# The experts of a mixture layer: gather behind gate/up, scatter inside its group, one tile of gathered tokens, 22 places for weights

## Chip, cores and metric

The kernel runs on one NeuronCore of a Trainium2 chip. The metric is device time of one execution, in microseconds (us); the number to compare is the median of several executions. Engines: PE is TensorE (matrix products, PEld its weight loads), DVE is VectorE, ACT is ScalarE, POOL is GpSimd, SP is SyncE, which here only issues DMAs.

## What is computed

Two networks in a row on 256 tokens of width 1024, batch 1. The first has two layers of gated linear attention, forgetting attention and a convolutional feed-forward; the second has one layer of windowed attention and a recurrent mixer, and ends with a mixture of experts. Only the mixture matters here: 32 experts in 4 groups, each token picks a group and in it the best two experts, and every expert is a gated feed-forward of width 256.

```python
    e_w, e_idx = lax.top_k(jax.nn.softmax(e_sel, axis=-1), TOP_K)
    e_w = e_w / jnp.sum(e_w, axis=-1, keepdims=True)
    weights = (g_w * e_w).astype(h.dtype)
    expert = (g_idx * EXPERTS_PER_GROUP + e_idx).reshape(-1)
    ...
    hg = lax.ragged_dot(xs, w_gate, sizes)
    hu = lax.ragged_dot(xs, w_up, sizes)
    ys = lax.ragged_dot(jax.nn.silu(hg) * hu, w_down, sizes)
    ...
        y = hierarchical_moe(h, ...)
        x = x + ga2 * rmsnorm(y, ln2_post[l])
```

## The kernel before

All weights stream from HBM in loads of 1 MiB (128 x 2048 fp32). `stream_load` (L145) issues the next load of one list on SP's queue into a place; `stream_done` (L160) gives a place back when its weight has been used, and at once issues the next load into it. So loads go in list order, and a load waits for the release of the place that it takes. For the experts there are 21 places: 5 in `ring`, 10 in `ring2` (8 of them shared with buffers of the stage before), 5 in `ring3` (L1687) and 1 in `ring3b` (L1729). The expert list (L286) has 96 loads: per group gate, up and down of each expert. The very last down weight comes in four parts.

The 32 experts are worked in 11 groups (`GROUPS`, L267), p = 0 to 10, of two or four experts: pairs for p = 0 to 3, 5 and 7, quads for 4, 6, 8, 9 and 10 (`LAST`). The first eight experts are fixed, the others come in the order of their load, which SP reads from a register. In a pair an expert has up to 64 token places, in a quad 32, so a group fills 128 columns or rows. Should an expert have more tokens than places, `dense` (L1979) does the rest behind a branch; here it is skipped.

The schedule is written by hand (`manual_schedule`): every engine works in program order. A group p passes through these steps:

- `onehots(p)` (L1741): DVE and ACT make the 0/1 matrix from tokens to places (PQ, PR). It also takes the tile XG[p] for the gathered tokens, from two tiles "xg0" and "xg1" in turn.
- `gather(p, q)` (L1764), q = 0 and 1: 8 products (16 instructions) pick the group's tokens out of `xv` into one PSUM bank; then four scalings, ACT, DVE, ACT, DVE, write four of the eight k tiles of XG[p]. The bank is "g", of which there is one.
- `gate_up(p)` (L1795): products of gate, then of up, into bank "gu"; the hook `between` puts work behind a certain k. Then ACT's silu and DVE's product give sg.
- `down_1` (L1817): two transposes of sg into a bank "dn" (there are two), and DVE's copy hm.
- `places(p)` (L1778): transposes of PQ into bank "g", PT by ACT, and the places' weights ws by DVE.
- `down_2(p, hm)` (L1825): products of the down weights, 512 columns at a time; `parts` splits the scaled result into yh (ACT) and yl (DVE), each 1024 columns wide.
- `scatter(p)` (L1868): 8 products add yh and yl to four y banks, which stay through the whole stage. PSUM has 8 banks: four y, two "dn", one "gu", one "g".

The order on TensorE in the loop (L2039) for 0 < p < LAST: gate; gather(p+1, 0); half of up; gather(p+1, 1); the other half of up; three quarters of scatter(p-1); down_1's transposes; the last quarter of scatter(p-1); places(p+1); the down products. In group 0 the gathers stand elsewhere: places(0), gather(1, 0), down_1's transposes, gather(1, 1), the down products, places(1). `by_rank` (L1950), a row of small DVE operations, follows down_1 in group 1; `most_over` (L1974), a transpose into "g" and a reduction, follows group 3.

The last group works its four experts two by two, since their weights come last; before it stand the branch and the transposes of the output gain `gbrow`. `keep_warm` (L1703) issues dummy products; 40 of them stand before the last down products. These come in quarters of 256 columns, each followed by `parts` and by the scatter of the quarter before. Behind that the result is normalised: squares (`last_sq`, ACT), the gain (`last_gain`, DVE), the root (`post_r`, DVE and POOL), the sum with the residual (`last_sum`, three on DVE, one on ACT and POOL), and four stores.

Of the kernel before, what the change touches and what calls it, by code (L numbers as in the profile page):

```python
# [20 lines left out]
EPS = 1e-6  # L21
# [13 lines left out]
def kernel(ctx: ExitStack, tc: tile.TileContext, a: dict, out: bass.AP, dump=None):  # L35
# [124 lines left out]
    def stream_done(key):  # L160

        del W["tiles"][key]
        stream_load(W["from"].pop(key))
# [1563 lines left out]

    t3 = sb_pool("t3", "right")
    ring3b = sb_pool("ring3b", "right")  # L1729
    stream_load((ring3b, 1))  # L1730
    p3 = ctx.enter_context(tc.tile_pool(name="p3", bufs=1, space=PSUM))

    def c3(tag, bufs, shape, dtype=F32):
        return t3.tile([128] + list(shape), dtype, name=tag, tag=tag, bufs=bufs)
# [6 lines left out]
    def onehots(p):  # L1741

        n, x0 = len(GROUPS[p]), GROUPS[p][0]
        m = 128 // n
        PR[p] = c3("PR", 1, (2, 128))
        if p == 0:
            for i in range(2):
                for s in range(n):
                    dve.tensor_scalar(PR[p][:, i, m * s:m * s + m], it[:, 1, 0:m], pos[:, i, x0 + s:x0 + s + 1],
                                      ss[:, i, 7:8], op0=OP.is_equal, op1=OP.mult)  # L1750
        PQ[p] = c3("P", 2, (2, 128), F32R)
        ps_ = (pos if x0 < FIXED else posA)[:, :, x0:x0 + n]
        dve.tensor_tensor(PQ[p].rearrange("p i (a b) -> p i a b", a=n),
                          it[:, 1, None, None, 0:m].to_broadcast([128, 2, n, m]),
                          ps_[:, :, :, None].to_broadcast([128, 2, n, m]), op=OP.is_equal)
        for i in range(2) if p else ():
            r = ss[:, i, 7:8]
            if i:
                act.activation(PR[p][:, i], PQ[p][:, i].bitcast(F32), AF.Copy, scale=r)
            else:  # L1760
                dve.tensor_scalar(PR[p][:, i], PQ[p][:, i].bitcast(F32), r, None, op0=OP.mult)
        XG[p] = c3("xg%d" % (p % 2), 1, (8, 128))

    def gather(p, q, tag="g"):  # L1764
        pg = b3(tag, 2 if tag == "dn" else 1, (4, 128))
# [26 lines left out]
            r = slice(m * s, m * s + m)  # L1792
            dve.tensor_reduce(WS[p][r], pt[r, 256 + 2 * s:258 + 2 * s], axis=AX.X, op=OP.add)

    def gate_up(p, between):  # L1795
        n_ = len(GROUPS[p])
        m = 128 // n_
        pg = b3("gu", 1)

        for c0, n in ((0, "gate"), (256, "up")):  # L1800
            for s0 in range(0, n_, 2) if p == LAST else (0,):
                some = range(s0, s0 + 2 if p == LAST else n_)
                for k in range(8):
                    for s in some:
                        pe.matmul(pg[m * s:m * s + m, c0:c0 + 256], XG[p][:, k, m * s:m * s + m],  # L1805
                                  W["tiles"][3, n, GROUPS[p][s]][:, k * 256:k * 256 + 256], start=k == 0, stop=k == 7,
                                  skip_group_check=True)
                    if (n, k) in between:
                        between[n, k]()
                for s in some:  # L1810
                    stream_done((3, n, GROUPS[p][s]))
        sg = c3("sg", 1, (256,))
        act.activation(sg, pg[:, 0:256], AF.Silu)
        dve.tensor_tensor(sg, sg, pg[:, 256:512], op=OP.mult)
        return sg
# [8 lines left out]

    def down_2(p, hm):  # L1825
        m = 128 // len(GROUPS[p])
        yh, yl = c3("yh", 1, (1024,), F32R), c3("yl", 1, (1024,), F32R)
        YG[p] = (yh, yl)

        def products(pd, group, c0, c1):  # L1830
            pd = pd.rearrange("p (a b) -> p a b", b=256)
            for f in range(2):
                for s in group:
                    r = slice(m * s, m * s + m)
                    w = W["tiles"][3, "down", GROUPS[p][s]].rearrange("p (q f m) -> p q f m", q=4, f=2)
                    pe.matmul(pd[r], hm[:, f, r], w[:, c0 // 256:c1 // 256, f], start=f == 0, stop=f == 1,  # L1836
                              skip_group_check=True)

        def parts(pd, c0, c1):
            act.activation(yh[:, c0:c1], pd, AF.Copy, scale=WS[p])  # L1840
            dve.scalar_tensor_tensor(yl[:, c0:c1], pd, WS[p], yh[:, c0:c1].bitcast(F32), op0=OP.mult, op1=OP.subtract)  # L1841

        n = len(GROUPS[p])
        if p < LAST:
            for d in range(2):
                pd = b3("dn", 2)
                products(pd, range(n), d * 512, d * 512 + 512)
                parts(pd, d * 512, d * 512 + 512)
            for x in GROUPS[p]:
                stream_done((3, "down", x))  # L1850
            return

        pds = [b3(t, 2 if t == "dn" else 1) for t in ("dn", "dn", "gu", "g")]
        keep_warm(40, pds[0][:, 256:384])
        for q in range(4):
            products(pds[q][:, 0:256], range(n - 2), q * 256, q * 256 + 256)
        for q in range(4):
            products(pds[q][:, 0:256], range(n - 2, n), q * 256, q * 256 + 256)
            if q:
                scatter(p, range(4), q - 1)  # L1860
            parts(pds[q][:, 0:256], q * 256, q * 256 + 256)
            if q == 2:
                last_sq(0, 0), last_gain(0, 0)
        scatter(p, range(4), 3)

    LAST = len(GROUPS) - 1

    def scatter(p, some=range(4), q=None):  # L1868
        for c in some:
            i, d = c // 2, c % 2  # L1870
            if q is not None and d != q // 2:
                continue
            r = slice(0, 512) if q is None else slice(q % 2 * 256, q % 2 * 256 + 256)
            for n, part in enumerate(YG[p]):
                pe.matmul(y[i][d][:, r], PT[p][:, i * 128:(i + 1) * 128], part[:, d * 512 + r.start:d * 512 + r.stop],  # L1875
                          start=p == 0 and n == 0, stop=p == LAST and n == 1, skip_group_check=True)

    y = [[b3("y%d%d" % (i, d), 1) for d in range(2)] for i in range(2)]

# [22 lines left out]
    def ranks(step):  # L1902

        sq_ = [128, NV, NV]
        cmp = t3.tile(sq_, F32, name="cmp", tag="yh" if step else "yl", bufs=1) if step < 2 else W["cmp"]
        if step == 0:
            dve.tensor_tensor(cmp, key[:, None, :].to_broadcast(sq_), key[:, :, None].to_broadcast(sq_), op=OP.is_gt)
            dve.tensor_reduce(rank, cmp, axis=AX.X, op=OP.add)
# [70 lines left out]
    def dense():  # L1979
# [5 lines left out]
        dve.tensor_tensor(wov, pos, cap[:, None].to_broadcast([128, 2, 32]), op=OP.is_gt)  # L1985
        dve.tensor_tensor(wov, wov, wf, op=OP.mult)
        for i in range(2):
            h2T = t3.tile([128, 8, 128], F32, name="h2T", tag="xg%d" % (1 - LAST % 2), bufs=1)
            for k in range(8):
                z = t3.tile([128, 128], F32, name="z", tag="sg", bufs=1)  # L1990
                pz = b3("g", 1, (128,))
# [34 lines left out]
        tt[i, d] = W["res"][:, 2 * i + d].rearrange("p (a b) -> p a b", a=4)  # L2026
        dve.tensor_tensor(tt[i, d], y[i][d].rearrange("p (a b) -> p a b", a=4), gbrow[:, 4 * d:4 * d + 4], op=OP.mult)  # L2027

    def last_sum(i, d, eng):
        xd = xv[:, i, 4 * d:4 * d + 4]  # L2030
        if eng is pool:
            act.activation(tt[i, d], tt[i, d], AF.Copy, scale=ss[:, i, 3:4])
            pool.tensor_tensor(tt[i, d], tt[i, d], xd, op=OP.add)
        else:
            dve.scalar_tensor_tensor(tt[i, d], tt[i, d], ss[:, i, 3:4], xd, op0=OP.mult, op1=OP.add)  # L2035
        o = out[0, i * 128:(i + 1) * 128, d * 512:(d + 1) * 512].rearrange("p (a b) -> p a b", a=4)
        (act if d else sp).dma_start(o, tt[i, d])

    for p in range(len(GROUPS)):  # L2039
        if p == LAST:  # L2040
            most = nc.values_load(over[0:1, 0:1], min_val=0, max_val=256)
            with tc.If(most > 0):
                dense()

            gbrow = t3.tile([128, 8, 128], F32, name="gbrow", tag="xg%d" % (1 - p % 2), bufs=1)
            for q in range(2):
                pt = b3("g", 1, (4, 128))
                for c in range(4):
                    pe.transpose(pt[:, c], gains[:, 3, 4 * q + c:4 * q + c + 1].to_broadcast([128, 128]), ident)  # L2049
                act.activation(gbrow[:, 4 * q:4 * q + 4], pt, AF.Copy)  # L2050
        between = {}
        if 0 < p < LAST:
            onehots(p + 1)
            between = {("gate", 7): lambda: gather(p + 1, 0), ("up", 3): lambda: gather(p + 1, 1)}
        sg = gate_up(p, between)
        if p:
            scatter(p - 1, range(3))
        else:
            places(0), gather(1, 0, "dn")
        hm = down_1(sg)  # L2060
        if p:
            scatter(p - 1, range(3, 4))
        if p == 1:
            mx = by_rank()
        if p == 0:
            gather(1, 1)
        elif p < LAST:
            places(p + 1)
        down_2(p, hm)
        if p == 0:  # L2070
            places(1)
        if p == 3:
            most_over(mx)

    for i, d in ((1, 0), (0, 1), (1, 1)):
        last_sq(i, d)
    last_gain(1, 0)
    post_r(0, 0, True), post_r(1, 0, True)
    last_gain(0, 1)
    post_r(0, 0, False)  # L2080
    last_gain(1, 1)
    post_r(1, 0, False)
    last_sum(0, 0, dve), last_sum(0, 1, pool), last_sum(1, 0, dve), last_sum(1, 1, dve)


def _laid_out(v):
# [67 lines left out]
```

## Time and profile before

| what | value |
|---|---|
| median of 3 runs | 1057.34 us (1056.49 to 1057.43) |
| profiled execution, its own time | 1056.19 us |
| its span | 1054.4 us |
| PE busy | 1020.2 us (97%) |
| PEld busy | 901.8 us (86%) |
| DVE, ACT, POOL busy | 718.0 us (68%), 515.1 us (49%), 225.8 us (21%) |
| HBM read, mean rate | 246.23 MB, 235 GB/s |

The span is what the profiler saw of the program; the run's own time has some 1.8 us around it. A busy PE is not PE at its peak. In the timelines a row is a run of equal instructions: start, length, engine, line, operation, what it writes and reads, count, and in brackets how long its engine stood idle before it and what ended that. Products of fp32 count as two instructions. The granted clock of TensorE has two levels, shown as 1.00 (2.4 GHz) and 0.50 (1.2 GHz).

### The profile page before, as it was taken

Reading aid. Unit: us, or ns where it says so; the run is one execution under the profiler, and the core shown is the slowest. Engines: PE = TensorE matmul, PEld = TensorE weight load, DVE = VectorE, ACT = ScalarE, POOL = GpSimd, SP = SyncE. Lnnn points to the kernel's source line nnn. Section 1 sums busy time; section 2 is a strip of 40 time slices with the busy share of each in tenths; the row PEclk is TensorE's granted clock in tenths of the full one; section 3 lists DMA queues with packets and bytes.
Section 4 is the critical chain, followed back from the end, with each engine's and each line's share of the span. In section 5 each row is a group of like instructions: output and inputs, shape, how many; then the busy total and the mean of one; then the engine's idle time right before and its main releaser. Section 6 shows DMA issues by size and latency. Waiting matters only on the chain. (4 is left out here: it accounts for less than half of the span.)

```text
span 1054.4 us, 21292 instructions
## 1 busy us (share of the span) xinstructions
PE 1020.2 (97%) x8476; PEld 901.8 (86%) x8476; DVE 718.0 (68%) x1512; ACT 515.1 (49%) x914; POOL 225.8 (21%) x194
## 2 busy tenths in 40 slices
PE   8999999999999999999999999989999999999986
PEld 7989899999999998999999999988887766566543
DVE  6756778999988475677999999785666642222213
ACT  5554456666644554445666655566554322222212
POOL 2304122122112230322111213455323000000001
PEclk9999999999999999999999999999999999999988
DMA  8423155556678432334666659753258899999993
GB/s 326 171 81 120 59 210 206 211 215 225 231 259 317 176 137 81 121 120 163 234 214 249 224 218 343 276 211 123 82 203 353 352 350 364 390 419 420 420 420 142
DMA packets 36743, 248.69 MB, mean 236 GB/s; under 512 B 4240, under 2 KB 4672, under 8 KB 7840
## 3 DMA queue, kind: packets, MB, share of 16 engines
q1 hardware_dynamic: 35616, 245.53, 61.5%
q8 instruction: 68, 1.11, 0.4%
q10 hardware_dynamic: 864, 1.37, 0.4%
q0 software_dynamic: 160, 0.39, 0.1%
q14 instruction: 35, 0.29, 0.1%
HBM read 246.23 MB, written 1.05 MB: 235 GB/s over the span
## 5 line engine op out<-in xcount | busy, mean ns | idle before, releaser
L211 PE MATMUL mm<-xh,wh 128*128 128x272 f32 (+1 forms) x1192 | 348.6, 292 | 3.0 <-DVE raw L1491 1.3
L214 PE MATMUL mm<-xh,wl 128*128 128x272 f32 (+1 forms) x1192 | 341.0, 286 | 0.0
L212 PE MATMUL mm<-xl,wh 128*128 128x272 f32 (+1 forms) x1192 | 340.0, 285 | 0.0
L182 ACT ACTIVATE wh<-raw 128x1024 fp32r<-128x1024 f32 (+1 forms) x229 | 237.9, 1041 | 144.9 <-PE mm L212 85.8
L191 POOL TENSOR_TENSOR wl<-raw,wh 128x1024 fp32r<-128x1024 f32 (+1 forms) x68 | 164.1, 2413 | 487.1 <-ACT wh L182 472.7
L211 PEld LDWEIGHTS mm<-xh,wh 128*128 128x128 f32 x1192 | 225.7, 189 | 13.2 <-issue 11.1
L191 DVE TENSOR_TENSOR wl<-raw,wh 128x1024 fp32r<-128x1024 f32 (+1 forms) x162 | 196.1, 1213 | 44.0 <-ACT wh L182 42.8
L214 PEld LDWEIGHTS mm<-xh,wl 128*128 128x128 f32 x1192 | 225.9, 189 | 0.0
L212 PEld LDWEIGHTS mm<-xl,wh 128*128 128x128 f32 x1192 | 225.5, 189 | 0.0
L1805 PE MATMUL gu<-raw,xg 128*32 128x256 f32 (+1 forms) x1024 | 91.6, 392 | 2.1 <-DMA raw<-in_w_exp_up_dram 2.1
L1023 DVE SCALAR_TENSOR_TENSOR cv<-lg,vcol,cv 128x256 f32<-128x256 f32 (+2 forms) x168 | 81.8, 487 | 3.0
L1805 PEld LDWEIGHTS gu<-raw,xg 128*32 128x32 f32 (+1 forms) x1024 | 49.6, 122 | 38.4 <-issue 4.7
L211 PE MATMUL lg<-big,wh 128*128 128x272 f32 (+2 forms) x240 | 68.3, 285 | 0.0
L212 PE MATMUL lg<-big,wh 128*128 128x272 f32 (+2 forms) x240 | 68.2, 284 | 0.0
L214 PE MATMUL lg<-big,wl 128*128 128x272 f32 (+2 forms) x240 | 68.1, 284 | 0.0
L1774 DVE TENSOR_SCALAR xg<-g,gains,modT 128x128 f32<-128x128 f32 x40 | 16.4, 410 | 74.6 <-ACT xg L1776 74.6
L1012 ACT ACTIVATE cv<-lg,vcol 128x272 f32<-128x272 f32 (+1 forms) x84 | 47.5, 565 | 36.7 <-DVE lg L1010 36.5
L211 PE MATMUL mm<-big,wh 128*128 128x272 f32 (+2 forms) x208 | 59.4, 286 | 0.0
L212 PE MATMUL mm<-big,wh 128*128 128x272 f32 (+2 forms) x208 | 59.1, 284 | 0.0
L214 PE MATMUL mm<-big,wl 128*128 128x272 f32 (+2 forms) x208 | 59.0, 284 | 0.0
L1616 POOL TENSOR_TENSOR ss<-ss,nhalf 128x1 f32<-128x1 f32 x6 | 3.7, 624 | 233.2 <-DVE ss L1614 230.0
L1776 ACT ACTIVATE xg<-g,modT,gains 128x128 f32<-128x128 f32 x40 | 18.3, 458 | 68.6 <-PE g L1768 59.0
(538 smaller groups left out, 1771.3 us busy)
## 6 DMA issues: line engine op xcount, KB each, us to landing
raw<-in_w_up_dram SPq DMA_DIRECT2D x44, 1024.0 KB, 4.8
raw<-in_w_in_dram SPq DMA_DIRECT2D x34, 1024.0 KB, 4.8
raw<-in_w_exp_gate_dram SPq DMA_DIRECT2D x32, 1024.0 KB, 10.6
raw<-in_w_exp_up_dram SPq DMA_DIRECT2D x32, 1024.0 KB, 11.1
raw<-in_w_exp_down_dram SPq DMA_DIRECT2D x31, 1024.0 KB, 12.5
raw<-in_w_ada_dram SPq DMA_DIRECT2D x24, 1024.0 KB, 4.8
raw<-in_w_down_dram SPq DMA_DIRECT2D x16, 1024.0 KB, 5.7
raw<-in_w_out_dram SPq DMA_DIRECT2D x12, 1024.0 KB, 4.8
```

The source lines that it names most:

```text
L182: act.activation(wh, src, AF.Copy)
L191: eng.tensor_tensor(wl, src, wh.bitcast(F32), op=OP.subtract)
L211: pe.matmul(po, wh[:, k - off], xh[:, tsl], start=f, stop=False)
L212: pe.matmul(po, wh[:, k - off], xl[:, tsl], start=False, stop=False)
L214: pe.matmul(po, wl[:, k - off], xh[:, tsl], start=False, stop=e)
L1012: act.activation(t, hs[:, D0:NN], AF.Identity, bias=conv_bias(l, c), scale=conv_col(l, 2, c))
L1023: dve.scalar_tensor_tensor(o, i, conv_col(l, j, c), o, op0=OP.mult, op1=OP.add)
L1616: pool.tensor_tensor(ss[:, i, c + 3:c + 4], ss[:, i, c + 2:c + 3], nhalf[:, :1], op=OP.pow)
L1774: dve.tensor_scalar(XG[p][:, k], pg[:, c], g, bb, op0=OP.mult, op1=OP.add)
L1776: act.activation(XG[p][:, k], pg[:, c], AF.Identity, bias=bb, scale=g)
L1805: pe.matmul(pg[m * s:m * s + m, c0:c0 + 256], XG[p][:, k, m * s:m * s + m], W["tiles"][3, n, GROUPS[p][s]][:, k * 256:k * 256 + 256], star ...
```

## The change

- `ring3b` has two places instead of one (22 in all), and both are loaded at the start.
- XG is one tile "xg" for all groups. gather(p+1, 0) stands behind gate_up(p), ahead of down_1 and places(p+1); in group 0 places(0) stands ahead of it, now in the same bank "g".
- In `down_2` both "dn" banks are taken first; the first half is split into yh and yl (512 columns wide now, one tile each) between the products; then come scatter of the first half, `parts` of the second, gather(p+1, 1), scatter of the second half. The scatter of group p-1 inside group p is gone.
- In the last group 14 dummies stand behind gate/up in place of 40 before down_2; three quarters of the down products of the first two experts come ahead, the fourth is done with all four experts; the second half of yh and yl takes the tile "xg".
- `h2T` and `gbrow` move to a place of the ring that has become free; `cmp` in `ranks` is bf16.
- At the end the squares of the first halves come earlier, the root needs one DVE operation less behind the last square, and all four sums are on DVE.

```diff
-    stream_load((ring3b, 1))
+    for _ in range(2):
+        stream_load((ring3b, 2))
...
-        XG[p] = c3("xg%d" % (p % 2), 1, (8, 128))
+        XG[p] = c3("xg", 1, (8, 128))
...
-    def gate_up(p, between):
+    def gate_up(p):
...
-                    if (n, k) in between:
-                        between[n, k]()
...
         def parts(pd, c0, c1):
+            c0, c1 = c0 % 512, (c1 - 1) % 512 + 1
+            if c0 == 0 and p == LAST and p in YG:
+                both = c3("xg", 1, (2, 512), F32R)
+                YG[p] = [both[:, 0], both[:, 1]]
+            elif c0 == 0:
+                YG[p] = [c3(t, 1, (512,), F32R) for t in ("yh", "yl")]
...
         if p < LAST:
+            pds = [b3("dn", 2) for _ in range(2)]
             for d in range(2):
-                pd = b3("dn", 2)
-                products(pd, range(n), d * 512, d * 512 + 512)
-                parts(pd, d * 512, d * 512 + 512)
+                products(pds[d], range(n), d * 512, d * 512 + 512)
+                if d == 0:
+                    parts(pds[d], 0, 512)
             for x in GROUPS[p]:
                 stream_done((3, "down", x))
+
+            scatter(p, 0)
+            parts(pds[1], 512, 1024)
+            gather(p + 1, 1)
+            scatter(p, 1)
             return
...
-        keep_warm(40, pds[0][:, 256:384])
-        for q in range(4):
+        for q in range(3):
             products(pds[q][:, 0:256], range(n - 2), q * 256, q * 256 + 256)
         for q in range(4):
-            products(pds[q][:, 0:256], range(n - 2, n), q * 256, q * 256 + 256)
+            products(pds[q][:, 0:256], range(n - 2, n) if q < 3 else range(n), q * 256, q * 256 + 256)
             if q:
-                scatter(p, range(4), q - 1)
+                scatter(p, (q - 1) // 2, (q - 1) % 2)
             parts(pds[q][:, 0:256], q * 256, q * 256 + 256)
-            if q == 2:
-                last_sq(0, 0), last_gain(0, 0)
-        scatter(p, range(4), 3)
+            if q > 1:
+                last_sq(q - 2, 0), last_gain(q - 2, 0)
+        dve.tensor_scalar(ss[:, :, 2], ss[:, :, 0], 1.0 / 1024, EPS, op0=OP.mult, op1=OP.add)
+        scatter(p, 1, 1)
...
-        cmp = t3.tile(sq_, F32, name="cmp", tag="yh" if step else "yl", bufs=1) if step < 2 else W["cmp"]
+        cmp = t3.tile(sq_, BF, name="cmp", tag="yh" if step else "yl", bufs=1) if step < 2 else W["cmp"]
...
-            between = {("gate", 7): lambda: gather(p + 1, 0), ("up", 3): lambda: gather(p + 1, 1)}
-        sg = gate_up(p, between)
-        if p:
-            scatter(p - 1, range(3))
+        sg = gate_up(p)
+        if p == LAST:
+            keep_warm(14, b3("dn", 2, (128,)))
         else:
-            places(0), gather(1, 0, "dn")
+            if p == 0:
+                places(0)
+            gather(p + 1, 0)
         hm = down_1(sg)
-        if p:
-            scatter(p - 1, range(3, 4))
         if p == 1:
             mx = by_rank()
-        if p == 0:
-            gather(1, 1)
-        elif p < LAST:
+        if p < LAST:
             places(p + 1)
         down_2(p, hm)
-        if p == 0:
-            places(1)
...
-    last_sum(0, 0, dve), last_sum(0, 1, pool), last_sum(1, 0, dve), last_sum(1, 1, dve)
+    last_sq(0, 1), last_sq(1, 1)
     last_gain(0, 1)
...
+    for i in range(2):
+        dve.scalar_tensor_tensor(ss[:, i, 3:4], ss[:, i, 1:2], 1.0 / 1024, ss[:, i, 2:3], op0=OP.mult, op1=OP.add)
+        pool.tensor_tensor(ss[:, i, 3:4], ss[:, i, 3:4], nhalf[:, :1], op=OP.pow)
+        if i == 0:
+            last_gain(1, 1)
+    for i in range(2):
+        for d in range(2):
+            last_sum(i, d)
```

## Rows read from the trace of the kernel before

**Rows 1.** Windows: us; busy of PE, PEld, DVE, ACT, POOL; PEclk, DMA share, GB/s.

```profile
846.30:899.15 52.85, 52.68 (x381) 34.05 (x380) 18.67 (x59) 13.05 (x29) 0.00 (x0) 1.00 0.92 353
916.75:987.17 70.42, 70.17 (x668) 43.97 (x668) 20.55 (x54) 17.45 (x36) 0.00 (x0) 1.00 1.01 420
987.17:1009.69 22.52, 20.39 (x210) 11.47 (x202) 5.30 (x15) 4.36 (x9) 0.00 (x0) 0.92 1.02 421
```

**Rows 2.** SP queue's waits, 846 to 910, then 920 to 1005: total, times, longest.

```profile
SPq L155 <- PE gu L1805: 22.6, 7, 5.6
...
SPq L155 <- DMA raw<-in_w_exp_down_dram: 13.9, 11, 1.5
```

**Rows 3.** Timeline of TensorE, group 2 (863.85 to 881.34 us).

```profile
863.85 3.62 PE L1805 MATMUL gu<-raw,xg 128*64 128x256 f32 x32
867.40 2.05 PE L1768 MATMUL g<-PR,hT 128*128 128x128 f32 x16
...
875.24 0.50 PE L1875 MATMUL y<-yh,PT 128*128 128x512 f32 x1
...
876.74 0.38 PE L1820 MATMUL dn<-ident,sg 128*128 128x128 f32 x2
...
877.43 0.38 PE L1784 MATMUL g<-ident,P 128*128 128x128 f32 x2
...
877.86 3.65 PE L1836 MATMUL dn<-raw,hm 128*64 128x512 f32 x16
881.34 3.62 PE L1805 MATMUL gu<-raw,xg 128*64 128x256 f32 x32
```

**Rows 4.** Timeline of all engines in group 0, around gather(1, 0).

```profile
837.89 2.03 PE L1768 MATMUL dn<-PR,hT 128*128 128x128 f32 x16
...
838.47 0.33 DVE L1793 TENSOR_REDUCE ws<-g 64x1 f32<-64x2 f32 x2
...
839.96 0.46 ACT L1776 ACTIVATE xg<-dn,modT,gains 128x128 f32<-128x128 f32 x1 [1.52 <-PE dn L1768]
...
841.39 0.41 DVE L1774 TENSOR_SCALAR xg<-dn,gains,modT 128x128 f32<-128x128 f32 x1 [0.53 <-ACT xg L1776]
841.72 0.41 DVE L1822 COPY hm<-dn 128x256 f32<-128x256 f32 x1
...
842.23 0.65 PE L1836 MATMUL dn<-raw,hm 128*64 128x512 f32 x2 [0.31 <-issue]
```

**Rows 5.** Timeline of DVE in group 1: by_rank's first operation, and both yl behind it.

```profile
860.01 0.16 DVE L1952 COPY proc<-it 128x8 f32<-128x8 f32 x1
...
864.13 1.43 DVE L1841 SCALAR_TENSOR_TENSOR yl<-dn,ws,yh 128x512 fp32r<-128x512 f32 x2
```

**Rows 6.** Timeline of TensorE: waits of an earlier stage, and those of group 9.

```profile
700.25 0.36 PE L211 MATMUL mm<-xh,wh 128*128 128x258 f32 x1 [0.34 <-DVE raw L1491]
...
702.97 0.65 PE L1217 MATMUL at<-ident,gains 128*128 128x128 f32 x4 [1.04 <-DVE gains L1205]
...
993.60 0.62 PE L1805 MATMUL gu<-raw,xg 128*32 128x256 f32 x2 [0.25 <-DMA raw<-in_w_exp_up_dram]
996.09 3.34 PE L1805 MATMUL gu<-raw,xg 128*32 128x256 f32 x26 [1.87 <-DMA raw<-in_w_exp_up_dram]
```

**Rows 7.** Windows of TensorE alone: us; busy; PEclk, DMA share, GB/s.

```profile
996.50:999.80 3.30, 3.30 (x27) 0.50 1.02 425
```

**Rows 8.** The chain that ended last, from the last group on.

```profile
1016.26 13.92 PE gu L1805 x128
1030.18 1.59 PE y L1875 x6
...
1032.46 2.25 PE dn L1706 x40
1034.71 1.85 PE dn L1836 x16
...
1047.67 1.75 DVE raw L2035
```

More of the change, by code (lines that the diff above doesn't have):

```diff
@@ L1826, in down_2 @@
         m = 128 // len(GROUPS[p])
-        yh, yl = c3("yh", 1, (1024,), F32R), c3("yl", 1, (1024,), F32R)
-        YG[p] = (yh, yl)
         def products(pd, group, c0, c1):
@@ L1839, in parts @@
         def parts(pd, c0, c1):
+            c0, c1 = c0 % 512, (c1 - 1) % 512 + 1
[4 more added lines that the diff above has]
+                YG[p] = [c3(t, 1, (512,), F32R) for t in ("yh", "yl")]
+            yh, yl = YG[p]
             act.activation(yh[:, c0:c1], pd, AF.Copy, scale=WS[p])
@@ L1859, in down_2, with scatter @@
             if q:
-                scatter(p, range(4), q - 1)
+                scatter(p, (q - 1) // 2, (q - 1) % 2)
             parts(pds[q][:, 0:256], q * 256, q * 256 + 256)
-            if q == 2:
-                last_sq(0, 0), last_gain(0, 0)
-        scatter(p, range(4), 3)
+            if q > 1:
+                last_sq(q - 2, 0), last_gain(q - 2, 0)
+        dve.tensor_scalar(ss[:, :, 2], ss[:, :, 0], 1.0 / 1024, EPS, op0=OP.mult, op1=OP.add)
+        scatter(p, 1, 1)
     LAST = len(GROUPS) - 1
[L1868 to L1873, printed above, removed]
+    def scatter(p, d, q=None):
+        r = slice(0, 512) if q is None else slice(q * 256, q * 256 + 256)
+        for i in range(2):
@@ L1874, in scatter @@
             for n, part in enumerate(YG[p]):
-                pe.matmul(y[i][d][:, r], PT[p][:, i * 128:(i + 1) * 128], part[:, d * 512 + r.start:d * 512 + r.stop],
-                          start=p == 0 and n == 0, stop=p == LAST and n == 1, skip_group_check=True)
+                pe.matmul(y[i][d][:, r], PT[p][:, i * 128:(i + 1) * 128], part[:, r], start=p == 0 and n == 0,
+                          stop=p == LAST and n == 1, skip_group_check=True)
     y = [[b3("y%d%d" % (i, d), 1) for d in range(2)] for i in range(2)]
@@ L1987, in dense @@
         for i in range(2):
-            h2T = t3.tile([128, 8, 128], F32, name="h2T", tag="xg%d" % (1 - LAST % 2), bufs=1)
+            h2T = spare[:, 0:1024].rearrange("p (a b) -> p a b", a=8)
             for k in range(8):
@@ L2027, in last_gain, with last_sum @@
         dve.tensor_tensor(tt[i, d], y[i][d].rearrange("p (a b) -> p a b", a=4), gbrow[:, 4 * d:4 * d + 4], op=OP.mult)
-    def last_sum(i, d, eng):
+    def last_sum(i, d):
         xd = xv[:, i, 4 * d:4 * d + 4]
[L2031 to L2035, printed above, removed]
+        dve.scalar_tensor_tensor(tt[i, d], tt[i, d], ss[:, i, 3:4], xd, op0=OP.mult, op1=OP.add)
         o = out[0, i * 128:(i + 1) * 128, d * 512:(d + 1) * 512].rearrange("p (a b) -> p a b", a=4)
@@ L2040 @@
         if p == LAST:
+            spare = raw_tile(*R1)
             most = nc.values_load(over[0:1, 0:1], min_val=0, max_val=256)
@@ L2043 @@
                 dense()
-            gbrow = t3.tile([128, 8, 128], F32, name="gbrow", tag="xg%d" % (1 - p % 2), bufs=1)
+            gbrow = spare[:, 1024:2048].rearrange("p (a b) -> p a b", a=8)
             for q in range(2):
@@ L2050 @@
                 act.activation(gbrow[:, 4 * q:4 * q + 4], pt, AF.Copy)
-        between = {}
         if 0 < p < LAST:
             onehots(p + 1)
-            between = {("gate", 7): lambda: gather(p + 1, 0), ("up", 3): lambda: gather(p + 1, 1)}
-        sg = gate_up(p, between)
-        if p:
-            scatter(p - 1, range(3))
-        else:
-            places(0), gather(1, 0, "dn")
+        sg = gate_up(p)
+        if p == LAST:
+            keep_warm(14, b3("dn", 2, (128,)))
+        else:
+            if p == 0:
+                places(0)
+            gather(p + 1, 0)
         hm = down_1(sg)
-        if p:
-            scatter(p - 1, range(3, 4))
         if p == 1:
             mx = by_rank()
-        if p == 0:
-            gather(1, 1)
-        elif p < LAST:
+        if p < LAST:
             places(p + 1)
         down_2(p, hm)
-        if p == 0:
-            places(1)
         if p == 3:
             most_over(mx)
[L2075 to L2078, printed above, removed]
+    last_sq(0, 1), last_sq(1, 1)
     last_gain(0, 1)
-    post_r(0, 0, False)
-    last_gain(1, 1)
-    post_r(1, 0, False)
-    last_sum(0, 0, dve), last_sum(0, 1, pool), last_sum(1, 0, dve), last_sum(1, 1, dve)
+    for i in range(2):
[3 more added lines that the diff above has]
+            last_gain(1, 1)
+    for i in range(2):
+        for d in range(2):
+            last_sum(i, d)
 def _laid_out(v):
```

## The prediction

> **What bounds the kernel now.** I read the page first, then the experts' stretch (830 to 1054 us) by windows, then the DMA queue's waits, then TensorE's timeline of one group, then the timeline around the one place in the old kernel where the new order already occurs, and last the chain that ends the span.
>
> The windows show two regimes [rows 1]. In the pair groups (846 to 899 us) TensorE is busy without a break, 52.68 of 52.85 us, and the DMA moves 353 GB/s; from 917 us it moves 420 GB/s, its full rate here, while TensorE is still busy, 70.17 of 70.42 us. The queue's waits say the same: first SP waits for TensorE to release a place, later for earlier transfers [rows 2]. So the stage is close to balanced: a load of 1.05 MB costs 2.5 us at 420 GB/s, a pair group of six loads 15 us; one group costs TensorE 17.5 us (863.85 to 881.34) [rows 3]. TensorE first runs out of weights in group 9, which takes 22.52 us instead of 17.5 [rows 1, 3]. These 5.0 us are all the slack that TensorE has; what it loses beyond them moves the end.
>
> How it stays busy is seen in one group [rows 3]: a quarter gather of eight products (two of them per group, 2.0 us each) is cut into gate/up, and the up products behind it hide what ACT and DVE do with its result.
>
> **The 22nd place.** One load more in front is worth at most 2.5 us of DMA, and only where the DMA sets the end. It costs one issue on SP's queue, with nothing urgent behind it. I count it at nothing, because by the next part TensorE sets the end.
>
> **Gather behind gate/up.** Group 0 of the old kernel has this order once [rows 4]. The gather starts at 837.89 and ends 2.03 us later, at 839.92. Its four tiles are then scaled by ACT and DVE in turn (they read one PSUM bank, and each starts when the one before has ended): the first at 839.96, the fourth at 841.39, ended at 841.80, which is 1.88 us after the gather. Only then does DVE, in program order, copy hm (841.72 to 842.13), and the down products start at 842.23, 2.31 us after the gather's end. There a second gather of 2 us covers this, and 0.31 us of idle time is left [rows 4]. In the new order no second gather stands there. Behind the gather TensorE has two transposes (0.22 us), then places(p+1), whose transposes need the same bank "g" (one buffer), thus wait for the fourth scaling, and then the products, which wait for hm. With places at 0.43 us [rows 3] the products start 1.93 + 0.43 = 2.36 us after the gather; TensorE works 0.65 of it. **The new idle time is 1.71 us in each of groups 0 to 9, 17.1 us together.** I see nothing that takes this gap: sg is ready during the gather, and everything else stands behind the products in TensorE's order.
>
> In group 0 places(0) comes ahead of gather(1,0) in the same bank, so the gather waits for DVE's ws (838.47 + 0.33) instead of starting at 837.89: +0.95 us; the old 0.31 us goes [rows 4].
>
> **Scatter by halves in the group.** The number of products is the same. The first half waits for yl of the first half; ACT and DVE need some 1.5 us for it (a pass of DVE is 0.72 us, two take 1.43 [rows 5], and ACT's is about as long), beside the second half's products, 1.8 us of the 3.5 [rows 3]: nothing. The second yh reuses the first's tile and so waits for the first scatter, but gather(p+1,1), 2.0 us, stands between: nothing. The scalings behind that gather are covered by the second scatter (four products, 1.0 us: six take 1.5) and by the first four k of gate (1.8 us of 3.55) [rows 3]: nothing. Two exceptions. In group 1 DVE has by_rank in front of yl: from 860.01 to 864.13 [rows 5], 4.1 us, begun as hm's copy ends, so yl(0) ends about 4.6 us behind the products' start where scatter's second product wants it at 3.8: +0.8 us. In group 3 most_over's transpose needs bank "g" right behind the second scatter, 1.0 us before the scalings are through: +1.0 us. Group 9's own scatter, 2.0 us of work (1.59 us for six of eight [rows 8]), moves from the last group into group 9: +2.0 us there, and less behind.
>
> **One xg tile** costs nothing by itself: its first new write comes after gate/up has been read to the end. bf16 for cmp shortens work of DVE that nobody waits for: nothing.
>
> **Start of the last group.** 17.1 + 0.95 - 0.31 + 0.8 + 1.0 + 2.0 = 21.5 us more on TensorE, less the 5.0 us that it no longer waits for weights: +16.5 us. Weights are there by then. Their stream is delayed only up to the first release of group 4 (some 6.5 us, an estimate from the same terms, with one place more counted in); behind it the queue is full. The branch ahead of the last group and its own gate/up (6.57 us from 1009.69 to 1016.26, then 13.92 us [rows 1, 8]) stay as they are.
>
> **The last group.** From the end of gate/up (1030.18) to the first down products at 1034.71 it takes 4.53 us now: eight scatter products, transposes, forty dummies of 2.25 us [rows 8]. The new path has 14 dummies (14 x 0.056 = 0.8 us) over sg, transposes 0.2 us, and hm in 0.8 us (an estimate: a copy of 0.41 us [rows 4] and the hand-overs): 1.8 us, so -2.7 us. The first two experts' products fall from four quarters to three, -0.9 us; the last quarter takes all four experts at once, about +0.1 us, and a wait for scaling that used to be covered by work is a little longer, +0.2 us. Sum -3.3 us. In the old kernel these weights landed as they were needed; now they are there early, so nothing takes that back.
>
> **The end.** One sum went over ACT and POOL; beside it DVE's sum took 1.75 us [rows 8] against 0.72 us for a pass of that width with POOL at rest [rows 5]. Four sums in a row on DVE, with squares begun a step earlier: between 0 and -1.5 us, I take -0.8.
>
> **The clock.** After 1.87 us of waiting in group 9, with 0.25 us of idle time shortly ahead of it, 26 products took 3.34 us [rows 6] at a granted clock of 0.50, the 1.2 GHz level [rows 7]; at 2.4 GHz they take 26/64 of 3.6 us, 1.5 us. So a fall costs 1.9 us. A wait of 1.04 us with 0.34 us ahead of it [rows 6] was followed by products at full speed. The new gap of 1.7 us lies between 2.12 and 1.38, a little nearer to the second. Ends: none of ten gaps falls (0) or all do (19 us). I take one, +2 us.
>
> The Trainium skill ("TensorE: Matmul & The Clock Gate", section "Why this matters for your kernels") lets the clock fall only after a whole window of idle time; by that rule this term is 0 and the sum 2 us smaller. Group 9's row disagrees, since TensorE had worked 0.62 us between its two waits there, and the row decides.
>
> **Sum.** +16.5 - 3.3 - 0.8 + 2 = +14.4 us on the profiled execution's 1056.19 us: 1070.6. That execution lay 1.15 us under the median of the runs, 1057.34, so the median to expect is 1071.7, called 1072.
>
> **Rivals.**
> *The gap is covered and the DMA sets the end* (faster): if ACT and DVE scale while the gather runs, or in parallel, the down products start on time. Then the 22nd place gives its 2.5 us, the last group 3.3 and the tail 0.8: 1050.7 us. It decides from a gap under 0.26 us (4.4 us of other losses + ten gaps - 5.0 - 4.1 = -2.1). For it: ACT and DVE are idle most of the stretch. Against: all of the old kernel's gathers show the alternation, and with it even the 2 us cover left 0.31 us [rows 4]. Chance 0.10.
> *The clock falls at many of the gaps* (slower still): five to ten falls cost 9.5 to 19 us instead of 2: 1080 to 1089 us. For it: idle time of group 9 in a similar amount did it [rows 6, 7]. Against: a kept clock after 1.04 us. Chance 0.22.
> *The gap is there, but a third as long* (0.6 us), for instance because places gets its bank early: then the extra work is about the slack plus the last group's gain, 21.5 - 11 - 5.0 = 5.5, less 4.1: 1058.7, about the same. Chance 0.05.
> *The change doesn't do what it says*: the second load of the ring lands later than assumed. While TensorE sets the end this moves nothing; it is in the forecast.
>
> **Numbers.** Forecast as summed 0.63, with the rivals 0.22, 0.10 and 0.05. The forecast's own range is 1066 to 1076 (clock 0 to 3 falls, tail and exceptions). Taken to 1063 and 1084 it leaves out the faster rival and the upper half of the clock's. A measurement can tell 0.2%, 2.1 us, from no change: faster 0.11, same 0.03, slower 0.86.
>
> **What would show it.** Right: in each of groups 1 to 9 TensorE idle about 1.7 us between down_1's transposes and places' transposes, released by the fourth scaling; a pair group of about 19.2 us; no wait for weights in group 9; the first gate product of the last group near 1033 us; its down products 1.8 us behind gate/up. Wrong: groups of 17.5 us still, waits for weights at the end, or a granted clock of 0.5 behind most gaps.

## Result, and the profile after

The changed kernel takes 1069.82 us (median of 4 runs, 1067.67 to 1072.07) beside 1057.0 us for the kernel before on the same chip: ratio 1.0123, 95% interval 1.0098 to 1.0148. It is slower, 1072 was forecast, inside the range. The profiled execution took 1067.73 us with a span of 1066.0, 11.6 us more than the span before.

The windows of the changed kernel, one line for each of groups 0 to 9 (us; busy of PE, PEld, DVE, ACT, POOL; PEclk, DMA share, GB/s):

```profile
830.73:851.18 20.45, 17.76 (x132) 11.75 (x131) 9.21 (x29) 5.20 (x11) 0.00 (x0) 1.00 0.94 378
851.18:871.88 20.70, 18.92 (x127) 11.69 (x126) 8.19 (x32) 4.37 (x9) 0.00 (x0) 0.92 0.80 307
871.88:892.60 20.72, 18.95 (x127) 11.69 (x126) 4.84 (x13) 4.37 (x9) 0.00 (x0) 0.92 0.80 304
892.60:914.59 21.99, 19.20 (x128) 11.77 (x127) 5.62 (x16) 4.82 (x10) 0.00 (x0) 0.92 0.80 305
914.59:933.57 18.98, 17.20 (x207) 10.71 (x207) 4.61 (x12) 3.91 (x8) 0.00 (x0) 1.00 0.85 341
933.57:954.28 20.71, 18.93 (x128) 11.69 (x127) 5.14 (x15) 4.37 (x9) 0.00 (x0) 0.92 1.01 422
954.28:973.27 18.99, 17.22 (x207) 10.71 (x207) 4.84 (x13) 4.37 (x9) 0.00 (x0) 1.00 1.01 420
973.27:992.28 19.01, 17.23 (x128) 11.29 (x127) 5.12 (x15) 4.37 (x9) 0.00 (x0) 1.00 1.01 420
992.28:1011.26 18.98, 17.21 (x208) 10.71 (x207) 5.13 (x15) 4.37 (x9) 0.00 (x0) 1.00 1.01 419
1011.26:1032.02 20.76, 18.96 (x207) 11.03 (x206) 5.22 (x15) 4.36 (x9) 0.00 (x0) 0.92 1.01 419
```

A group that took 17.5 us [rows 1, 3] takes 19.0 where the clock stays at 1.00 (groups 4, 6, 7, 8) and 20.7 where the mean is 0.92 (1, 2, 5, 9; group 3 has most_over's wait besides). PE is idle some 1.8 us of each line: TensorE is no longer busy without a break. In groups 1 to 3 the DMA moves 305 GB/s, where it moved 353 [rows 1]: places come free later (from 846 to 910 us SP's queue waits 48.9 us for TensorE's releases, before it was 39.7).

TensorE's waits in the changed kernel, 830 us to the end (engine, line, waited for: us in total, times, longest):

```profile
PE g L1785 <- DVE xg L1775: 17.8, 10, 1.8
PE g L2053 <- DVEq L2046: 1.7, 1, 1.7
PE g L1983 <- DVE xg L1775: 1.0, 1, 1.0
PE g L1769 <- DVE ws L1794: 0.9, 1, 0.9
PE g L2053 <- ACT raw L2054: 0.7, 1, 0.7
PE dn L1832 <- DVE hm L1821: 0.5, 1, 0.5
```

The first line is the whole stall: ten times 1.78 us, at the transposes of places, released by the last scaling of the gather. No wait for weights is left.

The timeline of all engines in group 2 of the changed kernel shows how the gap comes about:

```profile
878.94 2.05 PE L1769 MATMUL g<-PR,hT 128*128 128x128 f32 x16
...
880.83 0.38 PE L1819 MATMUL dn<-ident,sg 128*128 128x128 f32 x2
881.09 0.46 ACT L1777 ACTIVATE xg<-g,modT,gains 128x128 f32<-128x128 f32 x1 [1.62 <-PE g L1769]
881.58 0.41 DVE L1775 TENSOR_SCALAR xg<-g,gains,modT 128x128 f32<-128x128 f32 x1 [1.66 <-ACT xg L1777]
882.03 0.46 ACT L1777 ACTIVATE xg<-g,modT,gains 128x128 f32<-128x128 f32 x1 [0.48 <-DVE xg L1775]
882.52 0.41 DVE L1775 TENSOR_SCALAR xg<-g,gains,modT 128x128 f32<-128x128 f32 x1 [0.53 <-ACT xg L1777]
882.85 0.41 DVE L1821 COPY hm<-dn 128x256 f32<-128x256 f32 x1
...
882.99 0.44 PE L1785 MATMUL g<-ident,P 128*128 128x128 f32 x2 [1.77 <-DVE xg L1775]
...
883.18 0.36 PE L1787 MATMUL g<-w,P 128*128 128x4 f32 x2
```

Four scalings pass the bank from engine to engine, ACT, DVE, ACT, DVE, with hm behind the last, as in group 0 before [rows 4]; only the work that stood beside them is gone. What follows is slow here:

```profile
883.47 5.35 PE L1832 MATMUL dn<-raw,hm 128*64 128x512 f32 x16
888.75 0.50 PE L1882 MATMUL y<-yh,PT 128*128 128x512 f32 x1
```

The sixteen down products behind the gap take 5.35 us; they took 3.65 [rows 3]. In five of the ten groups the granted clock fell to its 1.2 GHz level at that place (in group 3 it is 0.52 from 904.20 to 907.50 us, in group 4 it is 1.00 from 926.17 to 929.70), 1.70 us each, 8.5 us together; behind the five other gaps, of the same length, it stayed at 2.4 GHz.

Where the 11.6 us of span lie, from the two timelines: the stage starts 0.3 later; groups 0 to 9 take 201.3 us (830.73 to 1032.0) instead of 179.3 (830.41 to 1009.69), +22.0; from there to the last gate/up 3.6 instead of 6.5, -2.9; the last gate/up 11.5 instead of 13.9, -2.4; from its end to the last scatter's end 11.0 instead of 14.3, -3.3; the rest 7.9 instead of 10.0, -2.1.

### The profile page after: what moved, and what is told of

The parts are those of the page before. It is cut to its first block, busy times and chain, and to the rows that moved or that the text cites. A ratio compares the mean times of both kernels' runs of the same rounds, so it can differ in the third digit from the quotient of the medians.

```text
span 1066.0 us, 21229 instructions
## 1 busy us (share of the span) xinstructions
PE 1018.4 (96%) x8450; PEld 899.6 (84%) x8450; DVE 716.9 (67%) x1512; ACT 514.4 (48%) x913; POOL 224.6 (21%) x193
## 5 line engine op out<-in xcount | busy, mean ns | idle before, releaser
L1806 PE MATMUL gu<-raw,xg 128*32 128x256 f32 (+1 forms) x1024 | 82.7, 380 | 0.0
L1813 DVE TENSOR_TENSOR sg<-sg,gu 128x256 f32<-128x256 f32 x11 | 4.6, 422 | 70.5 <-ACT sg L1812 70.5
L1832 PE MATMUL dn<-raw,hm 128*32 128x512 f32 (+2 forms) x256 | 48.7, 658 | 0.5 <-DVE hm L1821 0.5
```

## The experiments

Nine kernels. All medians stand beside the kernel before on the same chip.

**The two holds, one at a time and both.** The gap may come from the PSUM bank "g" (places needs it) or from DVE's order (hm behind the scalings).

a_hm_first (picked and scaled are the two halves of gather):

```diff
-            gather(p + 1, 0)
+            pg = picked(p + 1, 0)
         hm = down_1(sg)
+        if p < LAST:
+            scaled(p + 1, 0, pg)
```

> The changed kernel, with the copy of hm put ahead of the scalings of gather(p+1, 0); the transposes of the places still write the PSUM bank that the gather has just filled. Theory (two holds of about equal length on TensorE, the bank and hm, one behind the other): the places still wait until VectorE has scaled the last slice out of that bank, so the idle stretch stays at 1.5 to 1.8 us in each of groups 0 to 9, groups without a fall of the clock last 18.8 to 19.1 us, and the time is 1066 to 1072 us. Rival (the order on VectorE alone makes the gap): it shrinks to under 0.4 us, groups last about 17.4 us, and the time is 1050 to 1055 us.

b_places_dn:

```diff
-        pt = b3("g", 1, (256 + 2 * n,))
+        pt = b3("dn", 2, (256 + 2 * n,))
```

> The changed kernel, with the transposes of the places in the other PSUM bank, which the gather does not use; the copy of hm stays behind the scalings on VectorE. Theory: the places follow down_1 at once, and the idle stretch moves to the first down products, which wait for hm: still 1.4 to 1.8 us in each of groups 0 to 9, 1066 to 1072 us. Rival (the bank alone makes the gap): under 0.4 us, groups of about 17.4 us, 1050 to 1055 us.

c_both, the two together, with by_rank behind the scalings:

```diff
-            gather(p + 1, 0)
+            pg = picked(p + 1, 0)
         hm = down_1(sg)
-        if p == 1:
-            mx = by_rank()
         if p < LAST:
             places(p + 1)
+            scaled(p + 1, 0, pg)
+        if p == 1:
+            mx = by_rank()
```

> The changed kernel with the chain behind the gather taken out of TensorE's way: the gather's products, then down_1 with hm's copy, then places(p+1) in a bank "dn", and only then the four scalings. Theory (the exposed chain and the clock falls behind it cost the time): the idle time behind down_1 falls from 1.77 us to under 0.4 us, no granted clock of 0.50 between groups 1 and 9, a group takes 17.5 to 17.8 us, and the DMA sets the end again: 1047 to 1051 us. Rival (scatter inside the group, with its waits, is what costs): groups still take 18.5 us or more, 1060 to 1070 us. Rival (the DMA lost its rate through late releases): TensorE waits for weights in groups 8 to 10, 1055 us or more.

Measured: a 1069.08 us (two executions; 1.0108, 1.0088 to 1.0128), b 1060.38 (1.0027, 1.0015 to 1.0039), c 1054.19 (0.9967, 0.9953 to 0.9981). TensorE's waits from 830 us on, first a:

```profile
PE g L1790 <- DVE xg L1780: 17.7, 10, 1.8
```

then b:

```profile
PE dn L1832 <- DVE hm L1821: 18.2, 11, 1.8
```

then c:

```profile
PE y L1887 <- DVE yl L1849: 2.4, 1, 2.4
PE dn L1837 <- DVE hm L1826: 2.3, 11, 0.5
PE gu L1811 <- DMA raw<-in_w_exp_up_dram: 1.9, 1, 1.9
...
PE dn L1837 <- DMA raw<-in_w_exp_down_dram: 1.5, 1, 1.5
```

With either hold taken away the idle time stays at ten times 1.77 us: in a it stays at the transposes of places, in b it moves to the down products, which wait for hm. With both away 0.18 us a group is left and groups last 17.26 us. The gap is two holds of equal length one behind the other: removing one leaves it as long as it was. c is faster than the kernel before, though above the 1047 to 1051 expected: by_rank now holds yl in group 1 (2.40 us, and the clock falls there), and from group 9 on weights are late.

The time expected of b was missed by 6 us with its gap as expected. Its clock fell behind two of the ten gaps only, those that end at 842.27 and 862.85 us; the four falls of a are one fewer than in the changed kernel. The spans of the changed kernel and b differ by 6.6 us (1066.0 and 1059.4). Groups 0 to 9 take 7.0 us less in b: three falls fewer are 5.1 us, and the rest are groups that are shorter by some 0.16 (a quad without a fall lasts 18.82 against 18.98) and ws, which holds TensorE for 0.65 us in group 1 instead of 0.92 in group 0. The medians differ by 9.4, since two of the changed kernel's four executions stand at 1072 us and b's profiled one is its slowest.

**The clock alone.** e_fill puts dummies in the gap:

```diff
         if p < LAST:
+            keep_warm(30, b3("dn", 2, (128,)))
             places(p + 1)
```

> The changed kernel with 30 dummies (1.7 us) between down_1's transposes and places(p+1) in groups 0 to 9, so the gap stays as long but TensorE isn't idle in it. Theory (gaps cost 1.77 us each, and in addition 1.7 us where the clock falls behind one): no fall of the clock from group 1 to 9, groups of 19.0 us, by_rank's wait of some 0.8 us appears in group 1; 1059 to 1063 us, with less spread between executions. Rival (falls have another cause): falls as before, 1067 to 1072 us.

Measured: 1060.61 us (1.0037, 1.0024 to 1.0049); the theory held. Groups 1 and 2 of e_fill by windows:

```profile
851.20:871.06 19.86, 19.17 (x158) 13.01 (x156) 8.20 (x31) 4.37 (x10) 0.00 (x0) 1.00 0.89 335
871.06:890.09 19.03, 18.93 (x158) 13.01 (x156) 4.83 (x12) 4.36 (x10) 0.00 (x0) 1.00 0.81 313
```

Group 2 lasts as long as a group of the changed kernel without a fall, 19.03 us: the gap itself costs the same whether TensorE idles or works in it, and what dummies can give back is the clock, 1.00 on average from 830 to 1030 us: 9.2 us of the median, and 7.8 of the span (1066.0 to 1058.2), which is the five falls' 8.5 less 0.8 that comes to light in group 1. Group 1 is 0.83 us longer than group 2: this is by_rank's delay, which the half clock had covered in the changed kernel (the slowed products are 1.70 us longer).

**The scatter alone.** f_old_gather is the changed kernel with the gather back inside gate/up (and the old order in group 0), two xg tiles and 21 places:

```diff
-        XG[p] = c3("xg", 1, (8, 128))
+        XG[p] = c3("xg%d" % (p % 2), 1, (8, 128))
...
-            gather(p + 1, 1)
             scatter(p, 1)
...
+            between = {("gate", 7): lambda: gather(p + 1, 0), ("up", 3): lambda: gather(p + 1, 1)}
```

> The changed kernel with the gather alone put back into gate/up as before the change (two tiles xg, so 21 places; scatter by halves and the new last group stay). Theory: groups of 17.5 to 17.8 us, no gap; the DMA sets the end; what is left is the gain of the last group and the tail: 1049 to 1053 us. Rival (scatter by halves costs): groups of 18.5 us and more, 1058 us or more.

Measured: 1069.94 us (1.0132, 1.0108 to 1.0155). Missed by 17 us; the rival held. Group 2 of f_old_gather, TensorE:

```profile
883.49 0.44 PE L1820 MATMUL dn<-ident,sg 128*128 128x128 f32 x2 [0.96 <-DVE sg L1814]
...
884.44 3.65 PE L1833 MATMUL dn<-raw,hm 128*64 128x512 f32 x16 [0.18 <-DVE hm L1822]
...
889.77 0.51 PE L1884 MATMUL y<-yh,PT 128*128 128x512 f32 x1 [0.55 <-ACT yh L1844]
890.56 0.50 PE L1884 MATMUL y<-yl,PT 128*128 128x512 f32 x1 [0.28 <-DVE yl L1845]
```

Two of the 2.85 us by which a group is longer (20.45 against 17.6) are these four waits; the rest stands in no wait. The scatter that was moved had covered sg, and the scatter by halves needs gather(p+1, 1) between its halves to cover the second yh and yl. So the two moves hang together: the gather's new place is what pays for the scatter's.

**The gather alone.** i_gather_alone is the kernel before with nothing but this:

```diff
-            between = {("gate", 7): lambda: gather(p + 1, 0), ("up", 3): lambda: gather(p + 1, 1)}
         sg = gate_up(p, between)
+        if 0 < p < LAST:
+            gather(p + 1, 0)
...
         down_2(p, hm)
+        if 0 < p < LAST:
+            gather(p + 1, 1)
```

> The kernel before, with only the gather moved: gather(p+1, 0) behind gate_up, gather(p+1, 1) behind down_2; the scatter of group p-1 stays where it was, the old last group and the old end stay, 21 places. Theory (the gap is made by what stands right behind the gather in the change, and a scatter of products that are ready covers it): groups of 17.5 to 17.9 us, no idle stretch over 0.5 us, 1055 to 1059 us. Rival (the gather behind gate/up costs a gap whatever follows it): 18.9 to 20.7 us in each group, 1067 to 1085 us.

Measured: 1057.52 us (1.0004, 0.9994 to 1.0013), no change, as the theory had it. Groups 4 to 8 of i_gather_alone by windows:

```profile
899.99:985.40 85.41, 85.41 (x872) 54.71 (x871) 24.53 (x65) 20.89 (x43) 0.00 (x0) 1.00 0.99 405
```

TensorE is busy for all 85.41 us, five groups of 17.08 (ahead of them, in group 3, most_over waits 1.9 us, an idle stretch that the expectation had excluded): the scatter of the group before stands behind the gather and covers its scalings. So the gather behind gate/up costs nothing by itself; it even gains 0.5 us a group over 17.6. That gain turns into waits for weights at the end:

```profile
PE gu L1805 <- DMA raw<-in_w_exp_up_dram: 4.7, 3, 2.2
```

**The 22nd place.** d_both_21 is c_both with 21 places, and a tile of its own for what used the spare place:

```diff
-    for _ in range(2):
-        stream_load((ring3b, 2))
+    stream_load((ring3b, 1))
...
-            spare = raw_tile(*R1)
+            spare = c3("spare", 1, (2048,))
```

> c_both with 21 places (gbrow's tile then has memory of its own). Theory: with TensorE back under the DMA's time the place is worth what one load costs, 2.5 us, so this run is 2 to 3 us slower than c_both. Rival (a place is worth nothing, as releases set the pace only in the pair groups): within 0.5 us of c_both.

Measured: 1056.86 us (0.9995, 0.9985 to 1.0004), 2.67 us slower than c_both; the theory held. One load in front is worth about its 2.5 us of transfer where the DMA sets the end.

**The end alone.** h_end is the kernel before with no dummies ahead of the last down products, three quarters ahead instead of four, and the four sums on DVE:

```diff
-        keep_warm(40, pds[0][:, 256:384])
-        for q in range(4):
+        for q in range(3):
...
-    last_sum(0, 0, dve), last_sum(0, 1, pool), last_sum(1, 0, dve), last_sum(1, 1, dve)
+    for i in range(2):
+        for d in range(2):
+            last_sum(i, d, dve)
```

> The kernel before with only the end of the change: no dummies ahead of the last down products, three quarters of the first experts ahead instead of four, the sums of the last lines on VectorE alone. Groups 0 to 9 stay. Theory (the shorter branch and the faster last gate/up of the changed kernel come from where TensorE stands then and not from the edits of the end): the 6.6 us between group 9 and the last gate/up and the 13.9 us of that gate/up stay within 0.3; the first down products start 1.9 to 2.3 us earlier but the second pair still waits for the last weights, which land at about 1036.7, so the last scatter ends within 0.8 us of before; the tail is 1.5 to 2.3 us shorter: 1054.5 to 1056 us. Rival (the edits of the end give the whole 7.4 us that the changed kernel showed from branch to tail): 1049 to 1051 us.

Measured: 1053.81 us (0.9974, 0.9964 to 0.9984), a little better than the theory's range and far from the rival's. The last gate/up of h_end, TensorE:

```profile
1012.36 0.62 PE L2049 MATMUL g<-ident,gains 128*128 128x128 f32 x4 [2.79 <-PEq L2042]
1013.73 0.92 PE L2049 MATMUL g<-ident,gains 128*128 128x128 f32 x4 [0.75 <-ACT gbrow L2050]
1014.58 10.72 PE L1805 MATMUL gu<-raw,xg 128*32 128x256 f32 x98
1026.63 3.64 PE L1805 MATMUL gu<-raw,xg 128*32 128x256 f32 x30 [1.33 <-SPq L2042]
```

This gate/up begins 1.6 us earlier than before (1016.19), then waits 1.33 us, and ends where it ended (the first scatter product behind it starts at 1030.21, before at 1030.11). So a shorter branch or a faster clock there is worth nothing as long as TensorE runs up against the weights; in the changed kernel it came 19 us later and found them there. The expectation that the branch stays within 0.3 us was wrong, and so was "the last scatter within 0.8 us of before": no wait for weights stands in its last products (the very last weight comes in quarters, and each product needs only its own), and the chain from gate/up to the last scatter shrank by 2.6 us (11.7 against 14.3).

**A version that beats both.** g_late_rank is c_both with by_rank and most_over where other work covers them, most_over's transpose in bank "gu" instead of "g" (the edit against c_both):

```diff
+        if p == 2:
+            mx = by_rank()
         sg = gate_up(p)
...
-        down_2(p, hm)
-        if p == 3:
+        if p == 4:
             most_over(mx)
+        down_2(p, hm)
```

> The version without the bank's hold and with hm first (c_both), with by_rank moved to the start of group 2, where gate/up covers it, and most_over's transposes moved to group 4 behind the scalings. Theory: group 1 loses its 2.40 us of wait and the fall of the clock behind it, group 3 its 1.02 us; all of groups 0 to 8 last 17.2 to 17.7 us; the loads of the weights then set the end in part, and 3 to 5 us saved on TensorE become 2 to 5 us: 1048 to 1052 us. Rival (the loads set the end wholly): the same as c_both, 1053 to 1055 us, with longer waits for weights in groups 8 to 10.

Measured: 1049.86 us (0.993, 0.9913 to 0.9946), 7 us faster than the kernel before and within the theory's range. Groups 0 to 8 of g_late_rank by windows, and its waits for weights:

```profile
830.07:985.77 155.70, 154.22 (x1381) 100.42 (x1380) 53.57 (x153) 39.21 (x83) 0.00 (x0) 1.00 0.97 396
```

```profile
PE gu L1811 <- DMA raw<-in_w_exp_up_dram: 2.2, 2, 1.9
PE dn L1837 <- DVE hm L1826: 2.1, 10, 0.5
...
PE dn L1837 <- DMA raw<-in_w_exp_down_dram: 1.5, 1, 1.5
```

Nine groups in 155.7 us are 17.3 each, at full clock. TensorE then waits 3.7 us for weights: the DMA sets the end again.

## Why the prediction was right, point by point

The total came out right, and so did its largest term with its mechanism. But three terms were off by several us, one upward (clock, 6.5) and two downward (3.1 and 5.3); that they nearly cancel is luck. The last group's first gate product, for which the prediction named a time near 1033 us, came at 1035.6.

- *The new idle time is 1.71 us in each of groups 0 to 9, 17.1 us together*: 17.8 us, at the place and with the releaser named. That two holds make it was shown by a, b and c.
- *Group 0 +0.95 for ws*: 0.92 us. *most_over +1.0*: 1.01 us (group 3). *Scatter of group 9, +2.0*: two times four products, 2.1 us (929.74 to 930.77 and 932.48 to 933.57 in group 4).
- *by_rank +0.8*: not seen in the changed kernel; 0.83 us in e_fill. The step was right, and a fall of the clock hid it.
- *Slack of 5.0 us*: used up whole; no wait for weights is left.
- *One xg tile, scatter by halves: nothing*: no wait in the changed kernel belongs to them. For the scatter this rests on the cover that the step named, gather(p+1, 1): without it f_old_gather pays. That bf16 shortens cmp was wrong and cost nothing: its operations take 0.74 to 0.76 us in both kernels.
- A term was missing. A group without a fall lasts 19.0 us, not 17.6 + 1.77 = 19.4: gate/up in one piece and the two gathers take 10.7 us (914.59 to 923.53, 930.77 to 932.48), while cut into each other they took 11.4 (899.15 to 910.57 in the old group 4). With the rest of a group 0.4 us slower this leaves some 0.3 to 0.4 us a group, and i_gather_alone shows it by itself, 17.08 against 17.6.
- *The clock: I take one fall, +2 us*. **This term was mis-sized**: the price of a fall was right (1.70 us for 1.9), the number was not, five in the profiled execution, 8.5 us, and 9.2 us of the median by e_fill. The rival of many falls was right in its mechanism, with five falls of ten; its 1080 us did not come because of the missing term above and the next point.
- *The branch ahead of the last group and its own gate/up stay as they are*. **Wrong by 5.3 us.** The branch took 2.9 us less and gate/up 2.4 us less. Before, TensorE waited 3.71 us for its own sequencer there, and the clock was at half until 4.0 us into gate/up, which is some 2.0 of the 2.4 us (an estimate); after, it waits 1.74 us, the clock holds, and the weights are there. The row of TensorE behind the branch in the kernel before:

```profile
1013.40 1.00 PE L2049 MATMUL g<-ident,gains 128*128 128x128 f32 x4 [3.71 <-PEq L2042]
```

  Its window from there into gate/up (columns as above), and that of the changed kernel to the end of gate/up:

```profile
1013.60:1020.20 6.60, 5.85 (x28) 2.93 (x28) 0.00 (x0) 1.19 (x2) 0.00 (x0) 0.50 1.02 422
```

```profile
1033.74:1047.09 13.35, 12.66 (x136) 7.10 (x136) 0.00 (x0) 1.20 (x2) 0.00 (x0) 1.00 0.91 365
```

  The edits of the end don't give the short wait: h_end has them and waits 2.79 us. Nor does the later place in time: g_late_rank is at the branch at 1010.1 us, the kernel before at 1009.7, and g's row is

```profile
1011.86 0.62 PE L2058 MATMUL g<-ident,gains 128*128 128x128 f32 x4 [1.74 <-DVEq L2051]
```

  while a_hm_first comes at 1030.3 us and waits 2.42. What the later place gives is that the weights are there, against which h_end ran up. The waits of 3.71, 2.79, 2.67 (i_gather_alone) and 2.42 us were all followed by the half clock. Those of 1.74 us were followed by the full one in the changed kernel, b, c, e and g, as was the 0.63 us of f_old_gather, but by the half one in d_both_21 (0.51 from 1023.00 to 1026.20 us). So the 5.3 us were not to be counted on, and why the wait at the branch is long in one kernel and short in another stays open.
- *The last group -3.3*: 11.0 us against 14.3 from gate/up's end to the last scatter, -3.3. *Down products 1.8 us behind gate/up*: 1.96.
- *The end -0.8*: -2.05 us. About 1.0 is the sums' own path, which h_end shows too (8.9 us against 10.0); the other 1.1 us is the landing of the last store, from its issue on ACT's queue, first of the kernel before, then of the changed one (h_end has 3.2 as well):

```profile
out_dram<-raw ACTq DMA_DIRECT2D x1, 256.0 KB, 3.2
```

```profile
out_dram<-raw ACTq DMA_DIRECT2D x1, 256.0 KB, 2.1
```

Added up, from the 14.4 us predicted for the profiled execution: clock +6.5, gaps +0.7, by_rank -0.8, gate/up uncut -3.1 (what the groups leave), branch and gate/up -5.3, end -1.3, the small ones +0.4 together: 11.5, measured 11.6. The median of the runs rose by 12.8.

The Trainium skill ("Perfetto Trace Analysis", section "Identifying Performance Opportunities") says that the same gap repeated on the engine that should be saturated can mean too little PSUM or SBUF for the next tile. The trace agrees in half: the gap of 1.77 us stands at a transpose that needs the one buffer of bank "g", but b_places_dn, with another buffer, kept it.

## What to carry to other kernels

Before work is moved out of a place, read what it covers there: on either side of a move, list who waits for its result and what the bottleneck engine does meanwhile. A gap can have several holds of equal length, and an edit that takes one away then leaves it as long as it was; look for the next one before giving up the idea. And a term of zero for a stage further on ("stays as it is") is an assumption: here that stage waited less, ran at another clock and found its weights there, 5.3 us in all.

## What was not expected of the hardware

- Ten equal gaps of 1.77 us with nearly the same work between them were followed by a fall of the clock in some groups and not in others: five of ten in the changed kernel, four in a_hm_first, two in b_places_dn, and none where dummies filled them. At the branch the same wait of 1.74 us was followed by a fall in d_both_21 and by none in five other kernels. The length of the gap alone doesn't tell it. The executions of the changed kernel differ as well: two at 1067.7 us with a mean granted clock of 0.99, two at 1072 with 0.982 and 0.987. What decides was not settled.
- The Trainium skill ("TensorE: Matmul & The Clock Gate", section "Why this matters for your kernels") ties the fall to one whole window without work, and the gaps that it warns of are longer than those here. The trace disagrees: TensorE worked 17 of every 19 us, was idle 1.77 us at a stretch, and the clock fell five times.
- The same store of 256 KB on ACT's queue at the very end landed 2.1 us after its issue in the changed kernel and the seven built on it, and 3.2 or 3.3 in the kernel before and the two built on that (h_end, i_gather_alone), one profiled execution each. So it goes with the program, but not with the sums, which h_end has as the changed kernel has them; what makes the 1.1 us wasn't tried.
